# Every third MLP weight unit: its low part summed by an accumulating DMA instead of subtracted on VectorE

## The chip, the cores and the metric

The kernel runs on one core of one Trainium2 chip. The metric is device time of the whole launch in microseconds (us), and a change counts as faster or slower here when the time moves by more than 2%. The core has five engines that run side by side and wait for each other by semaphores: TensorE (PE; its weight loads are listed apart as PEld), VectorE (DVE), ScalarE (ACT), GpSimd (POOL) and SyncE (SP). Sixteen DMA engines move data between HBM and the on-chip SBUF; in this kernel SP issues the weight loads, ACT the results, and POOL a few loads of x.

## The reference

One decoder layer in float32, with 256 tokens and a model width of 2048: an RMS norm and one combined input projection; a causal attention of 8 heads and a gated linear recurrence of 8 heads beside it; sigmoid gates that merge the two; an output projection with a residual; and then the MLP, which is half of all weights:

```python
x = x + merged @ w_out
u = jax.nn.relu(_rmsnorm(x, mlp_norm_g) @ w_mlp1)     # 2048 -> 8192
return x + (u * u) @ w_mlp2                           # 8192 -> 2048
```

All weights are float32, and the result is wanted at about float32 accuracy.

## The kernel before, in words

**The stream of weight units.** All weights are cut into 248 units of 128 x 2048 float32, 1 MB each, that the kernel walks once, in order. Units 0 to 119 belong to the projections; units 120 to 247 are the MLP. The MLP is done in two halves of its width: 32 units of `w1` (120 to 151), 32 of `w2` (152 to 183), 32 of `w1` (184 to 215), 32 of `w2` (216 to 247).

**Two parts of each number.** TensorE multiplies in the type float32r, which keeps fewer bits than float32. So each weight is split in two float32r parts: `hi`, the weight rounded (L110, ScalarE), and `lo`, the weight minus `hi` (L111, VectorE). The activations are held the same way, high and low part side by side in 512 columns (`cat`). A product takes, for each of the 16 blocks of a unit, one matmul of `hi` with all 512 columns and one of `lo` with the 256 high columns (`ws`, L278 to L281). The first block of an accumulation takes `hi` first (L278), then `lo` (L279); the later blocks take `lo`, then `hi` (L281).

**What sets the order.** The function `unit()` hands out unit u and, ahead of that, asks for the load and for the split (`cut`) of unit u+2. `raw`, `hi` and `lo` have three buffers each, so the split of u+2 may write when TensorE has finished with unit u-1, and the load of a unit may start when the split of the unit three before it has read its `raw` buffer. Loads are issued on SP's queue (L90). Each engine runs its instructions in an order that the framework's scheduler fixes when the program is built, and that may differ from the order in which the code is written.

**The MLP beside the matmuls.** In a `w1` unit ScalarE copies the cross terms out of PSUM (`cross`, L292), VectorE adds and applies relu and the norm (L293, L618), ScalarE squares (L620) and rounds the high part (L305), VectorE takes the low part (L306). In the `w2` units VectorE adds the result to the residual (L639, L641, L644). POOL has nothing to do in the MLP.

Of the kernel before, what the change touches and what calls it, by code (L numbers as in the profile page):

```python
# [9 lines left out]
F32 = mybir.dt.float32  # L10
F32R = mybir.dt.float32r
I32 = mybir.dt.int32
AF = mybir.ActivationFunctionType
OP = mybir.AluOpType
AX = mybir.AxisListType

P = 128
T = 256
# [12 lines left out]
def layer_kernel(ctx: ExitStack, tc: tile.TileContext, xT, vecs, wv, wm, wg, wu, wo, w1, w2, cf, cm, out):  # L31
    nc = tc.nc
# [15 lines left out]
    def g4(s, shape=(P, 1024), dt=F32):  # L48
        return gp.tile(list(shape), dt, tag="g", name=uid(s))

    def s1(s, dt=F32, n=256):
        return sp.tile([P, n], dt, tag=f"s{n}", name=uid(s), bufs=6 if n == 256 else 3)

    def bank(s, pool=pp):
        return pool.tile([P, 512], F32, tag="b", name=uid(s))

# [1 line left out]
    units = []  # L58
    for u in range(16):
        units.append(wv[u])  # L60
# [13 lines left out]
    split = {}  # L74
# [3 lines left out]
    def pieces(u):  # L78
        n = 4 if u < 2 else 2 if u < 6 else 1
        w = UW // n  # L80
        return [slice(i * w, (i + 1) * w) for i in range(n)]
# [19 lines left out]
    def cut(u):  # L101
        if u >= len(units):
            return
        hi = wp.tile([P, UW], F32R, tag="hi", name=f"hi{u}")
        lo = wp.tile([P, UW], F32R, tag="lo", name=f"lo{u}")
        raw = raws[u]
        for s in pieces(u):
            if u < 4:
                parts_of_x(range(4 * u + s.start // 512, 4 * u + s.stop // 512))
            nc.scalar.activation(hi[:, s], raw[:, s], AF.Copy)  # L110
            nc.vector.tensor_sub(lo[:, s], raw[:, s], hi[:, s].bitcast(F32))  # L111
        split[u] = (hi, lo)

    AHEAD = 2
# [2 lines left out]
    def unit():  # L117
        u = done[0]
        done[0] += 1
        load(u + AHEAD)  # L120
        cut(u + AHEAD)
        return split.pop(u)

# [1 line left out]
    side = []  # L125
    budget = [0.0]

# [14 lines left out]
                if next(s, None) is None:  # L142
                    side.remove(s)

# [1 line left out]
    NV = 16 + 16 + 32 + 3 + 16  # L146
    vt = cp.tile([P, NV], F32, name="vt")
    nc.scalar.dma_start(vt, vecs)
# [31 lines left out]
    lsc_t = cp.tile([P, 1], F32, name="lsc_t")  # L180
    nc.vector.memset(lsc_t, float(-0.5 * np.log(128.0)))

# [1 line left out]
    xcat = catp.tile([P, KD, 512], F32R, tag="cat", name="xcat")  # L184

    def parts_of_x(ks):
        for k in ks:
            src = xr[k // 4][:, k % 4, :]
            nc.scalar.activation(xcat[:, k, :T], src, AF.Copy, scale=g_in[:, k : k + 1])  # L189
            nc.vector.scalar_tensor_tensor(  # L190
                xcat[:, k, T:], src, g_in[:, k : k + 1], xcat[:, k, :T].bitcast(F32), op0=OP.mult, op1=OP.subtract
            )

    for u in range(2):
        cut(u)

    def rms_rows(ps, dst, n):
        nc.scalar.activation(dst, ps, AF.Sqrt, scale=1.0 / n, bias=eps_t)
        nc.vector.reciprocal(dst, dst)
# [3 lines left out]
    lb = cp.tile([P, 2, NH], F32, name="lb")  # L203

    def prepare():
        """The rms of x over the features, per token: on all partitions, and by partition;
        then the lower bound of the recurrence's gates."""
        acc = g4("acc", (P, 4, T))
        for c in range(4):
            if c == 0:  # L210
                nc.scalar.activation(acc, xr[0], AF.Square)
            else:
                sq = g4("xsq", (P, 4, T))
                nc.scalar.activation(sq, xr[c], AF.Square)
                nc.vector.tensor_add(acc, acc, sq)
            if c % 2:
                yield 1.2 * c
        ssum = cp.tile([P, T], F32, name="ssum")
        nc.vector.tensor_reduce(ssum, acc.rearrange("p k t -> p t k"), axis=AX.X, op=OP.add)
        yield 1.2  # L220
        ps = bank("ps_ss")
        for t in range(2):
            nc.tensor.matmul(ps[:, t : t + 1], ssum[:, t * P : (t + 1) * P], ones[:, :1], start=True, stop=True)
        rms_rows(ps[:, :2], rcol, D)
        ps = bank("ps_ss")
        nc.tensor.matmul(ps[:, :T], ones, ssum, start=True, stop=True)
        rms_rows(ps[:, :T], rstd, D)
        yield 2.2
        lbm = cp.tile([P, NH], F32, name="lbm")
        lbe = cp.tile([P, 2, NH], F32, name="lbe")  # L230
        nc.vector.tensor_max(lbm, lbl[:, 0, :], lbl[:, 1, :])
        for i in range(2):
            nc.vector.tensor_sub(lbe[:, i, :], lbl[:, i, :], lbm)
        nc.scalar.activation(lbe, lbe, AF.Exp)
        nc.vector.tensor_add(lbm, lbe[:, 0, :], lbe[:, 1, :])
        nc.vector.reciprocal(lbm, lbm)
        nc.vector.tensor_mul(lb[:, 0, :], lbe[:, 0, :], lbm)
        nc.vector.tensor_scalar(lb[:, 1, :], lb[:, 0, :], -1.0, 1.0, op0=OP.mult, op1=OP.add)
        yield 1.0

# [1 line left out]
    vv, ii = [[g4(n, (P, 1024)) for _ in range(2)] for n in ("v", "i")]  # L242

    def leave(c, pst):
# [5 lines left out]
    for c in range(4):  # L250
        pst = [bank(f"pv{t}", pm) for t in range(2)]
        for q in range(4):
            hi, lo = unit()
            hi, lo = (x.rearrange("p (k f) -> p k f", k=4) for x in (hi, lo))
# [15 lines left out]
    leave(*full.pop())  # L270

    def ws(parts, pst=None):
        """One tile of features: parts is a list of (hi, lo, cat) 128 x 128 and 128 x 512."""
        pst = pst if pst is not None else bank("pw", pm)
        n = len(parts)
        for i, (h, l, cat) in enumerate(parts):
            if i == 0:
                nc.tensor.matmul(pst, h, cat, start=True, stop=False)  # L278
            nc.tensor.matmul(pst[:, T:], l, cat[:, :T], start=False, stop=False)  # L279
            if i > 0:  # L280
                nc.tensor.matmul(pst, h, cat, start=False, stop=(i == n - 1))  # L281
        return pst

    def unit_parts(hi, lo, cats, off=0):
        return [
            (hi[:, off + k * P : off + (k + 1) * P], lo[:, off + k * P : off + (k + 1) * P], c)
            for k, c in enumerate(cats)
        ]
# [8 lines left out]
    def project(dst):  # L297
        pst = ws(unit_parts(*unit(), xcats))
        s = s1("s")
        summed(pst, s)  # L300
        nc.vector.tensor_mul(dst, s, rstd)

    def to_parts(dst, src, lo_engine=None):
        """dst[..., :n] and dst[..., n:] take the two parts of src."""
        nc.scalar.activation(dst[0], src, AF.Copy)  # L305
        nc.vector.tensor_sub(dst[1], src, dst[0].bitcast(F32))  # L306

# [1 line left out]
    orc = [None] * NH  # L309
    oac = [None] * NH  # L310

# [102 lines left out]
        yield 0.1  # L414

    def head_rms(x, log_scale=0.0):
        """exp(log_scale) / rms over the partitions of x (P, 4, T), on all partitions."""
        sq = g4("sq", (P, 4, T))
        nc.scalar.activation(sq, x, AF.Square)
        yield 0.1  # L420
        sh = g4("sqh", (P, 4, T), F32R)
        nc.scalar.activation(sh, sq, AF.Copy)
        sl = g4("sql", (P, 4, T), F32R)
        nc.vector.tensor_sub(sl, sq, sh.bitcast(F32))
        yield 1.2
        for b in range(2):
            pb = bank("pb")
            hs = slice(2 * b, 2 * b + 2)
            nc.tensor.matmul(pb, ones_r, sh[:, hs, :], start=True, stop=False)  # L429
            nc.tensor.matmul(pb, ones_r, sl[:, hs, :], start=False, stop=True)  # L430
            nc.scalar.activation(
                sq[:, hs, :], pb.rearrange("p (h t) -> p h t", h=2), AF.Ln, scale=1.0 / P, bias=eps_t
            )
        nc.scalar.activation(sq, sq, AF.Exp, scale=-0.5, bias=log_scale)
        yield 0.1
        return sq
# [11 lines left out]
                orc[4 * g + 2 * b + j] = oc[:, j, :]  # L448
        yield 1.2

# [1 line left out]
    shuf = [(i + 16) % 32 for i in range(32)]  # L452

    def rotate(x):
# [92 lines left out]
                step()  # L547
        side.append(attend(g, q, k))

# [1 line left out]
    ga = []  # L551
    for j in range(KD):
        if j % 4 == 0:
# [6 lines left out]
    for j in range(KD):  # L560
# [5 lines left out]
        hi, lo = unit()  # L566
# [5 lines left out]
        a = s1("a")  # L572
# [5 lines left out]
        to_parts((mt[:, j % 2, :T], mt[:, j % 2, T:]), a)  # L578
        mcat.append(mt[:, j % 2, :])

# [1 line left out]
    x2 = []  # L582
    for c in range(4):
        t = g4("x2", (P, 4, T))
# [18 lines left out]
            nc.vector.tensor_add(acc2, acc2, sq)  # L603
    rstd2 = cp.tile([P, T], F32, name="rstd2")

# [1 line left out]
    x2cats = [x2cat[:, k, :] for k in range(KD)]  # L607
    for half in range(2):
        ucat = []
# [15 lines left out]
        for j in range(KD):  # L625
            parts = unit_parts(*unit(), ucat[:16]) + unit_parts(*unit(), ucat[16:])
# [43 lines left out]


def _ws(w):
    """(K, F) as tiles of 128 features: (F / 128, 128 of K, K / 128, 128)."""
    k, f = w.shape
    return np.ascontiguousarray(w.reshape(k // P, P, f // P, P).transpose(2, 1, 0, 3))

# [55 lines left out]
```

## Time and profile before

| | |
|---|---|
| time, two runs | 1456.84 and 1457.02 us, median 1456.93 us |
| profiled execution: span from first to last instruction | 1455.0 us |
| what lies around the span, from the median | 1.9 us |
| granted TensorE clock over the span | 1.000 |
| busy: PE, PEld, DVE, ACT, POOL | 100%, 87%, 62%, 47%, 0% of the span |
| bytes by DMA | 268.14 MB, mean 184 GB/s |
| chain that ended last | PE 99% of it |

The page does not give the profiled execution a time of its own apart from its span; the two timed runs lie 1.8 and 2.0 us above that span. Shares of busy time are taken over the span. The chain is the work followed back from the last instruction: an engine that is not on it can be busy and still cost nothing. An engine's idle time is listed with the instruction that ended it, its releaser.

### The profile page before, as it was taken

The numbers are of one execution on the slowest core, as the hardware profiler recorded it, in microseconds if no ns is written. First come the engines' busy times: TensorE is split into PE (matmuls) and PEld (weight loads), VectorE is DVE, ScalarE is ACT, GpSimd is POOL, SyncE is SP. The second block draws the span as 40 slices with busy tenths as digits, with TensorE's granted clock in tenths as the row PEclk, the third lists the DMA queues.
The fourth block names the chain that finished last, engine by engine and source line by source line (L and its number), as shares of the span: only waits on it lengthen the run. The fifth ranks groups of instructions, "written<-read, shape, count | busy, mean of one in ns | idle before, by whom it ended". The sixth has DMA issues, their size and how long they took to land.

```text
span 1455.0 us, 19682 instructions
## 1 busy us (share of the span) xinstructions
PE 1449.3 (100%) x8336; PEld 1261.7 (87%) x8336; DVE 899.0 (62%) x981; ACT 686.8 (47%) x778; POOL 4.4 (0%) x10
## 2 busy tenths in 40 slices
PE   9999999999999999999999999999999999999999
PEld 7888889888888888888888888888888888888888
DVE  8445776767876766767666666544445666654443
ACT  7444333565755545454455545333335555533331
POOL 0000000000000000000000000000000000000000
PEclk9999999999999999999999999999999999999999
DMA  9554443445444555554555545555545455555551
GB/s 333 204 201 174 173 146 134 156 147 200 150 169 174 173 190 214 190 215 176 192 185 177 200 175 196 179 198 178 198 178 193 183 185 192 177 210 190 208 190 68
DMA packets 41751, 268.14 MB, mean 184 GB/s; under 512 B 4768, under 2 KB 7072, under 8 KB 10688
## 3 DMA queue, kind: packets, MB, share of 16 engines
q1 hardware_dynamic: 38784, 262.78, 50.7%
q0 software_dynamic: 576, 2.10, 0.4%
q10 hardware_dynamic: 2304, 2.01, 0.4%
q8 instruction: 65, 1.06, 0.3%
q14 instruction: 22, 0.18, 0.0%
HBM read 264.78 MB, written 2.10 MB: 183 GB/s over the span
## 4 chain that ended last, share of the span: by engine, by line
PE 99%; DMA 0%; ACT 0%; DVE 0%; issue 0%
PE pw L281 56%; PE pw L279 30%; PE pw L278 3%; PE pv L260 2%; PE pv L262 2%; PE pv L261 2%; PE pd L357 1%; PE pl L485 0%; DMA raw<-wv 0%; PE pw L633 0%; PE pw L631 0%; PE pw L632 0%; PE pd L335 0%; PE pd L365 0%; PE pb L429 0%; PE pb L430 0%
## 5 line engine op out<-in xcount | busy, mean ns | idle before, releaser
L111 DVE TENSOR_TENSOR lo<-raw,hi 128x2048 fp32r<-128x2048 f32 (+2 forms) x258 | 569.3, 2208 | 287.5 <-ACT hi L110 287.3
L110 ACT ACTIVATE hi<-raw 128x2048 fp32r<-128x2048 f32 (+2 forms) x258 | 475.8, 1845 | 306.4 <-PE pw L281 225.6
L281 PE MATMUL pw<-xcat,hi 128*128 128x512 f32 x1080 | 383.6, 397 | 0.0
L281 PE MATMUL pw<-x2cat,hi 128*128 128x512 f32 x960 | 342.4, 399 | 0.0
L281 PE MATMUL pw<-ucat,hi 128*128 128x512 f32 x961 | 337.9, 396 | 0.0
L279 PE MATMUL pw<-xcat,lo 128*128 128x256 f32 x1152 | 311.2, 280 | 0.0
L279 PE MATMUL pw<-x2cat,lo 128*128 128x256 f32 x1024 | 277.2, 281 | 0.0
L279 PE MATMUL pw<-ucat,lo 128*128 128x256 f32 x992 | 271.6, 279 | 0.0
L292 ACT ACTIVATE cross<-pw 128x256 f32<-128x256 f32 x168 | 64.5, 384 | 421.2 <-PE pw L281 421.2
L281 PEld LDWEIGHTS pw<-xcat,hi 128*128 128x128 f32 x1080 | 202.8, 188 | 46.3
L279 PEld LDWEIGHTS pw<-xcat,lo 128*128 128x128 f32 x1152 | 217.5, 189 | 5.2
L281 PEld LDWEIGHTS pw<-ucat,hi 128*128 128x128 f32 x961 | 180.4, 188 | 42.1
L281 PEld LDWEIGHTS pw<-x2cat,hi 128*128 128x128 f32 x960 | 180.4, 188 | 42.0
L279 PEld LDWEIGHTS pw<-x2cat,lo 128*128 128x128 f32 x1024 | 193.5, 189 | 5.5
L279 PEld LDWEIGHTS pw<-ucat,lo 128*128 128x128 f32 x992 | 186.8, 188 | 2.8
L281 PE MATMUL pw<-mcat,hi 128*128 128x512 f32 x240 | 85.6, 399 | 0.0
L293 DVE TENSOR_TENSOR s<-pw,cross 128x256 f32<-128x256 f32 x72 | 30.4, 422 | 76.8 <-ACT cross L292 76.8
L293 DVE TENSOR_TENSOR t<-pw,cross 128x256 f32<-128x256 f32 x64 | 27.2, 426 | 76.3 <-ACT cross L292 76.3
L279 PE MATMUL pw<-mcat,lo 128*128 128x256 f32 x256 | 69.3, 281 | 0.0
L281 PEld LDWEIGHTS pw<-mcat,hi 128*128 128x128 f32 x240 | 45.1, 188 | 10.5
L260 PE MATMUL pv<-hi,xcat 128*128 128x512 f32 x128 | 49.3, 392 | 1.0 <-ACT xcat L189 1.0
L262 PE MATMUL pv<-hi,xcat 128*128 128x512 f32 x128 | 49.8, 389 | 0.0
(185 smaller groups left out, 1198.4 us busy)
## 6 DMA issues: line engine op xcount, KB each, us to landing
raw<-w SPq DMA_DIRECT2D x128, 1024.0 KB, 4.8
raw<-wm SPq DMA_DIRECT2D x56, 1024.0 KB, 4.8
raw<-wg SPq DMA_DIRECT2D x16, 1024.0 KB, 4.8
raw<-wu SPq DMA_DIRECT2D x16, 1024.0 KB, 4.8
raw<-wo SPq DMA_DIRECT2D x16, 1024.0 KB, 4.8
raw<-wv SPq DMA_DIRECT2D x10, 1024.0 KB, 4.8
raw<-wv SPq DMA_DIRECT2D x8, 512.0 KB, 6.9
raw<-wv SPq DMA_DIRECT2D x8, 256.0 KB, 5.1
```

What stands on the lines that cost most here:

```text
L110: nc.scalar.activation(hi[:, s], raw[:, s], AF.Copy)
L111: nc.vector.tensor_sub(lo[:, s], raw[:, s], hi[:, s].bitcast(F32))
L260: nc.tensor.matmul(pst[t], xh, hi[:, k, :], start=(kk == 0), stop=False)
L261: nc.tensor.matmul(pst[t], xh, lo[:, k, :], start=False, stop=False)
L262: nc.tensor.matmul(pst[t], xl, hi[:, k, :], start=False, stop=(kk == KD - 1))
L278: nc.tensor.matmul(pst, h, cat, start=True, stop=False)
L279: nc.tensor.matmul(pst[:, T:], l, cat[:, :T], start=False, stop=False)
L281: nc.tensor.matmul(pst, h, cat, start=False, stop=(i == n - 1))
L292: nc.scalar.activation(c, pst[:, T:], AF.Copy)
L293: nc.vector.tensor_add(dst, pst[:, :T], c)
L357: nc.tensor.matmul(pd[:, i * 64 : (i + 1) * 64].rearrange("p (n j) -> p n j", j=h2), ks[:, h, c], rhs, start=True, stop=True,)
```

## The change

`cut(u)` makes the low part in another way for every third unit of the MLP, u = 120, 123, ..., 246, which are 43 units. ScalarE writes `lo` as the raw weights times -1, rounded to float32r: that is `-hi`. Then a DMA issued by GpSimd reads the raw weights of the unit once more from HBM and adds them to what stands in `lo`. What is left there is the raw weight minus its rounded value, as before. For these units VectorE's subtraction is gone. All other units are cut as before. Some comments are dropped too; the line numbers after the change are 4 higher.

```diff
             nc.scalar.activation(hi[:, s], raw[:, s], AF.Copy)
-            nc.vector.tensor_sub(lo[:, s], raw[:, s], hi[:, s].bitcast(F32))
+            if u >= 120 and u % 3 == 0:
+                nc.scalar.activation(lo[:, s], raw[:, s], AF.Copy, scale=-1.0)
+                nc.gpsimd.dma_start(lo[:, s], units[u][:, s], accum_op=OP.add)
+            else:
+                nc.vector.tensor_sub(lo[:, s], raw[:, s], hi[:, s].bitcast(F32))
         split[u] = (hi, lo)
```

**ScalarE in a `w1` stretch.** Before, the order around the split of unit 132 (the names carry the unit, `hi132`; `cross_576` is the copy-out of unit 129):

```order
L292 ACTIVATE cross_571_6582<-pw_569_6548 128x256
L110 ACTIVATE hi131_6593<-raw131_6591 128x2048
L620 ACTIVATE u2_572_6586<-t_570_6581 128x256
L305 ACTIVATE ucat_573_6588<-u2_572_6586 128x256
L292 ACTIVATE cross_576_6631<-pw_574_6597 128x256
L110 ACTIVATE hi132_6641<-raw132_6639 128x2048
L620 ACTIVATE u2_577_6635<-t_575_6630 128x256
L305 ACTIVATE ucat_573_6588<-u2_577_6635 128x256
```

and the same place after the change:

```order
L296 ACTIVATE cross_571_6586<-pw_569_6552 128x256
L110 ACTIVATE hi131_6597<-raw131_6595 128x2048
L624 ACTIVATE u2_572_6590<-t_570_6585 128x256
L309 ACTIVATE ucat_573_6592<-u2_572_6590 128x256
L112 ACTIVATE lo132_6646<-raw132_6643 128x2048
L296 ACTIVATE cross_576_6635<-pw_574_6601 128x256
L110 ACTIVATE hi132_6645<-raw132_6643 128x2048
L624 ACTIVATE u2_577_6639<-t_575_6634 128x256
L309 ACTIVATE ucat_573_6592<-u2_577_6639 128x256
```

The negated copy (L112) stands ahead of the copy-out of unit 129 and of `hi132`, so `lo132` is written first and `hi132` after it.

**ScalarE in a `w2` stretch**, after the change, around the splits of units 162 and 165 (before, this is a plain row of L110, one for each unit):

```order
L110 ACTIVATE hi160_7959<-raw160_7957 128x2048
L110 ACTIVATE hi161_7965<-raw161_7963 128x2048
L112 ACTIVATE lo162_8039<-raw162_8036 128x2048
L110 ACTIVATE hi162_8038<-raw162_8036 128x2048
L110 ACTIVATE hi163_8045<-raw163_8043 128x2048
L110 ACTIVATE hi164_8118<-raw164_8116 128x2048
L112 ACTIVATE lo165_8125<-raw165_8122 128x2048
L110 ACTIVATE hi165_8124<-raw165_8122 128x2048
```

Here too the negated copy comes ahead of the high part of the same unit.

**GpSimd**, after the change: behind the four loads of x, which it had before, stand the 43 accumulating DMAs and nothing between them:

```order
L589 DMA x2_498_5409<-xT 128x1024
L589 DMA x2_499_5411<-xT 128x1024
L113 DMA lo120_6060<-w1 128x2048
L113 DMA lo123_6207<-w1 128x2048
L113 DMA lo126_6353<-w1 128x2048
```

The order on TensorE is the same as before; its first matmul with `lo` of such a unit now waits for a DMA where it waited for VectorE.

## Rows read from the trace of the kernel before

**Rows 1.** The page: busy us and share of each engine.
```profile
PE 1449.3 (100%) x8336; PEld 1261.7 (87%) x8336; DVE 899.0 (62%) x981; ACT 686.8 (47%) x778; POOL 4.4 (0%) x10
```

**Rows 2.** The page: the chain that ended last, by engine.
```profile
PE 99%; DMA 0%; ACT 0%; DVE 0%; issue 0%
```

**Rows 3.** The MLP as one stretch: length, busy us (instructions), PEclk, DMA share, GB/s.
```profile
core 0: us, PE busy (x) PEld busy (x) DVE busy (x) ACT busy (x) POOL busy (x), PEclk, DMA share, GB/s
735.00:1455.00 720.00, 716.79 (x4109) 624.68 (x4107) 392.03 (x384) 304.75 (x319) 0.00 (x0) 1.00 0.52 183
```

**Rows 4.** The split in the MLP, by line and shape: busy us, mean ns, idle before.
```profile
L111 DVE TENSOR_TENSOR lo<-raw,hi 128x2048 fp32r<-128x2048 f32 x126 | 288.9, 2293 | 194.8 <-ACT hi L110 194.8
...
L110 ACT ACTIVATE hi<-raw 128x2048 fp32r<-128x2048 f32 x125 | 239.1, 1913 | 224.7 <-PE pw L281 222.5 <-issue 2.2
```

**Rows 5.** Timeline of a `w1` stretch, TensorE: start us, us, instruction.
```profile
804.58 0.28 PE L279 MATMUL pw<-x2cat,lo 128*128 128x256 f32 x1
804.94 0.39 PE L278 MATMUL pw<-x2cat,hi 128*128 128x512 f32 x1
810.59 0.39 PE L278 MATMUL pw<-x2cat,hi 128*128 128x512 f32 x1
816.23 0.39 PE L278 MATMUL pw<-x2cat,hi 128*128 128x512 f32 x1
```

**Rows 6.** The same stretch, ScalarE and VectorE.
```profile
805.14 0.39 ACT L292 ACTIVATE cross<-pw 128x256 f32<-128x256 f32 x1 [2.71 <-PE pw L281]
805.42 1.91 ACT L110 ACTIVATE hi<-raw 128x2048 fp32r<-128x2048 f32 x1
807.23 0.40 ACT L620 ACTIVATE u<-t 128x256 f32<-128x256 f32 x1
807.66 0.42 ACT L305 ACTIVATE ucat<-u 128x256 fp32r<-128x256 f32 x1
...
807.36 2.29 DVE L111 TENSOR_TENSOR lo<-raw,hi 128x2048 fp32r<-128x2048 f32 x1 [0.92 <-ACT hi L110]
```

**Rows 7.** Timeline of a `w2` stretch at a unit's border.
```profile
1057.65 0.40 PE L281 MATMUL pw<-ucat,hi 128*128 128x512 f32 x1
...
1057.88 0.40 PE L278 MATMUL pw<-ucat,hi 128*128 128x512 f32 x1
...
1058.08 1.92 ACT L110 ACTIVATE hi<-raw 128x2048 fp32r<-128x2048 f32 x1 [3.73 <-PE pw L281]
...
1058.12 0.39 PE L279 MATMUL pw<-ucat,lo 128*128 128x256 f32 x2
```

**Rows 8.** The page, DMA queues: packets, MB, share of 16 engines' span.
```profile
q1 hardware_dynamic: 38784, 262.78, 50.7%
```

**Rows 9.** The page, DMA issues: line, engine, count, size of one, us to landing.
```profile
raw<-w SPq DMA_DIRECT2D x128, 1024.0 KB, 4.8
...
x<-xT POOLq DMA_DIRECT2D x4, 512.0 KB, 3.6
```

**Rows 10.** POOL's DMAs (tile x): duration ns min/median/max of the issue; then landing.
```profile
L585 POOL DMA_DIRECT2D x<-xT x4: 530/530/664, 508.1 to 636.3; - x4
...
DMA to landing us min/median/max: 3.4/3.6/4.5
```

**Rows 11.** One weight load, us by us, columns as in the rows of the MLP stretch.
```profile
804.00:805.00 1.00, 1.00 (x8) 0.86 (x7) 0.34 (x2) 0.00 (x0) 0.00 (x0) 1.00 0.06 8
805.00:806.00 1.00, 1.00 (x8) 0.87 (x7) 0.42 (x1) 0.86 (x2) 0.00 (x0) 1.00 0.73 147
806.00:807.00 1.00, 1.00 (x7) 0.91 (x6) 0.42 (x1) 1.00 (x1) 0.00 (x0) 1.00 1.05 442
807.00:808.00 1.00, 1.00 (x7) 0.86 (x7) 0.64 (x1) 0.97 (x3) 0.00 (x0) 1.00 0.99 418
808.00:809.00 1.00, 1.00 (x8) 0.86 (x7) 1.00 (x1) 0.08 (x1) 0.00 (x0) 1.00 0.14 49
```

**Rows 12.** Who waited for whom, SP's queue: us in total, times, longest us.
```profile
SPq L90 <- DVE lo L111: 727.9, 137, 11.4
SPq L90 <- DVE ucat L306: 351.9, 63, 6.2
```

## The prediction, made before the changed kernel ran

> **What bounds the kernel now.** I read the totals first, then the chain, then the MLP alone, where the whole change lies. TensorE is busy for 1449.3 of 1455.0 us [rows 1], and 99% of the chain that ended last is TensorE's [rows 2]. In the MLP it is busy 716.79 of 720 us at a granted clock of 1.00, that is 2.4 GHz [rows 3]. VectorE is busy there for 392 us and ScalarE for 305 us, and each spends its idle time waiting for what is ahead of it: the subtraction (L111) waits for the rounding (L110), and the rounding for TensorE [rows 4]. So nothing on VectorE sets the end. The idle time of TensorE in the whole span, 1455.0 - 1449.3 = 5.7 us or 0.4%, is all that relief for another engine can give back. The question is thus only whether the new way delivers `lo` in time; if it does not, TensorE stops at its first matmul with that `lo`, 43 times.
>
> **The time there is.** A unit lasts 5.65 us: TensorE's first matmuls of three units start at 804.94, 810.59 and 816.23 [rows 5]. With three buffers, `lo` of unit u+2 may be written when the last `lo` matmul of unit u-1 has ended, at 804.58 + 0.28 = 804.86 [rows 5], some 0.03 later for the hand-over (the rounding starts at 1058.08, the matmul that frees its buffer ends at 1057.65 + 0.40 [rows 7]). It is needed at the first `lo` matmul of unit u+2, at 816.23 plus the 0.24 between L278 and the first L279 (1057.88 to 1058.12 [rows 7]): 816.47. That is 11.6 us. Before, the rounding and the subtraction of a `w1` unit were done at 807.36 + 2.29 = 809.65 [rows 6], with 6.8 us to spare.
>
> **What is removed.** 43 subtractions of 2.293 us [rows 4], 98.6 us of VectorE. Worth nothing: VectorE is not on the chain.
>
> **What is added on ScalarE.** 43 negated copies. No such row exists; it has the form of the rounding, 128 x 2048 from SBUF to SBUF, so I take its 1.91 us [rows 4, 6]: 82 us on top of 305 of 720. In a `w1` unit ScalarE's work becomes 0.39 + 1.91 + 0.40 + 0.42 + 1.91 = 5.0 us [rows 6], under 5.65. The order shows the copy ahead of `cross` and of `hi`. So those come 1.9 us later: `hi` is done near 804.89 + 1.91 + 0.39 + 1.91 = 809.1, seven us ahead of its use, and the PSUM bank that `cross` empties is one of four. Cost: nothing, covered by that slack. The copy itself ends at 806.80.
>
> **What is added on GpSimd.** Behind the copy, POOL issues the DMA; its queue holds nothing else in the MLP, and an issue takes 0.53 us [rows 10], within the landing time. From 806.83 to 816.47, less a hand-over, **the DMA has 9.6 us from issue to landing.** In a `w2` stretch, when the unit is the second of its pair, `lo` is the first operand and the limit is 0.24 lower.
>
> **What the DMA takes.** No accumulating DMA stands in the trace, so I bound it. The weight loads take 0.507 x 1455.0 = 738 us of all 16 engines for 262.78 MB [rows 8], 2.94 us for 1 MB (1,048,576 bytes), and land after 4.8 us [rows 9]: 1.9 us of latency around the data. POOL's loads of half that size land after 3.6 us [rows 9, 10]: 1.47 of data and 2.1 around them.
> - Lower end: one read, alone: 2.1 + 2.94 = 5.1 us. Hidden by 4.5 us.
> - Two reads: an add needs the raw row from HBM and the standing row from SBUF, so I count the data twice, 5.88 us: 8.0 us alone.
> - Sharing: the weight load three units ahead is issued when `hi` has been written (809.1), 2.3 us behind this DMA. During such a load the DMA engines are full (share 1.05 and 0.99 at 442 and 418 GB/s [rows 11]), so it is not free. If the engines alternate row by row, the accumulating DMA, whose rows take twice as long, gets two thirds: 2.0 us alone, then the remaining 3.9 in 5.8 us, in sum 2.1 + 2.0 + 5.8 = 9.95 us. If the load goes first entirely: 2.1 + 5.88 + 2.94 = 10.95 us.
> - Upper end: two reads and the write one after another, 3 x 2.94 = 8.8 us, behind a load: 2.1 + 8.8 + 2.94 = 13.9 us.
>
> I take 9.95 us, since doubling the reads is the least that an add must do and the rows show both transfers on the same engines. The stall is 9.95 - 9.6 = 0.35 us, times 43 = 15 us. It does not add up from unit to unit, since the next split starts when TensorE moves on. Weight loads that come late cost nothing: issued at 809.1, needed 12.8 us later, when the split of the unit three on starts, they land after 4.8 us, and 5.88 more still fit. SP waits for VectorE before nearly every load [rows 12]; after the change it waits for ScalarE's `hi` (809.1) instead of `lo` (809.65), no later. Over three units (16.9 us) the engines would hold 3 x 2.94 + 5.88 = 14.7 us of data, so they do not saturate.
>
> **Sum:** 1456.9 + 15 = **1472 us**. The terms come from an execution with a span of 1455.0 us; the median 1456.93 lies 1.9 us above it, and I add to the median.
>
> **The skill beside this.** The sharing term rests on the full engines of [rows 11]. The Trainium skill, "DMA: Bandwidth & Descriptors", section "Issuing engines are not separate DMA queues", says the same against this change: DMAs of any issuing engine run on the same 16 and interleave. Were it otherwise, 8.0 us would be hidden and the sum 1457 us. For the price of the add only a page has figures: the Trainium skill, "Collectives: The Full Stack", section "The bandwidth ceiling: the fold count and why AG ≠ RS ≠ AR", says that a reducing DMA runs at half the copy's rate because it reads two sources, not because the add costs cycles, with about 31 GB/s read by one engine. By its figures an estimate is 1,048,576 x 2 / (16 x 31,000) = 4.2 us of data, 8.3 to 9.3 us with latency and load, and the sum would be 1457 us. No run here shows it yet.
>
> **Rivals.**
> 1. *The add costs more than two reads* (slower). Place: the wait of TensorE's first `lo` matmul on POOL's DMA. It decides from 9.6 us on, and 2% (29 us, 0.68 us a unit) is passed at 10.3. Ends: 10.95 us gives 43 x 1.35 = 58, 1515 us; 13.9 us gives 43 x 4.3 = 185, 1642 us. For it: the limit sits right at my estimate, and casting into float32r or a longer issue on POOL would each push it over. Against: only 14.7 of 16.9 us of engine time asked. 0.28.
> 2. *Rows are not overlapped* (much slower). 128 rows on 16 engines are 8 each; if each row waited for its own write, with 2.1 us each and the data of 2.94, 20 us: 43 x 10.4 = 447, 1904 us. The loads overlap theirs, which speaks against it, but an add must read, then write the same place. 0.19 for all above 14 us.
> 3. *Hidden altogether*: one read counts, or the load does not disturb: 1457 us. It is one case with my forecast, since less than 2% parts them; together 0.51, with a range of their own from 1452 to 1486 us.
> 4. *Faster*: only if matmuls themselves got shorter with VectorE quieter, since waits hold 0.4% at most. Nothing in the rows points to it: 0.02.
>
> **Range and chances.** Differences under 2%, about 29 us, count as no change. Low end 1450 us: the 5.7 us of idle time returned. High end 1640 us: rival 1 to its upper end; only rival 2 (0.19) and a little of rival 4 lie outside. Faster 0.02, same 0.51, slower 0.28 + 0.19 = 0.47.
>
> **What the profile after would show.** Right: POOL's 43 DMAs land some 10 us after issue, a quarter of DMA-engine time more in the MLP, L112 near 1.91 us, TensorE idle before L283 waiting for DMA for under 0.5 us each, clock still 1.00. Rival 1 or 2: the landing time above 10.3 us, TensorE's idle time near 43 times the excess. Rival 3: landing under 9.6 us and no wait of TensorE. The prediction is wrong in its first step if TensorE waits on ScalarE (`hi` or L112) instead, or if SP's loads come late and L110 waits for `raw`.

## The result, and the profile after

The changed kernel takes 1471.09 us (two runs, 1468.84 and 1473.33) against 1456.93 us: a ratio of 1.0091, 95% interval 1.0075 to 1.0107. That is slower beyond the noise and under the 2% that count as a change. The forecast was 1472 us. In the profiled execution (1468.84 us) the span is 1467.1 us, 12.1 us longer than before.

The page's totals, against [rows 1]:

```profile
PE 1455.2 (99%) x8336; PEld 1259.3 (86%) x8336; DVE 802.1 (55%) x938; ACT 763.8 (52%) x821; POOL 41.5 (3%) x53
```

VectorE lost 97 us and ScalarE gained 77 us, and neither shows in the time. The MLP as one stretch, against [rows 3]; the columns are the same:

```profile
735.00:1467.00 732.00, 722.95 (x4111) 622.47 (x4109) 297.71 (x342) 380.19 (x361) 36.16 (x42) 1.00 0.80 240
```

It is 12.0 us longer, which is the whole loss; the clock stays at 1.00. TensorE's idle time grew by 5.8 us only (720 - 716.79 before, 732 - 722.95 now) and its busy time by 6.2 us for the same matmuls. A matmul that waits at its start is partly drawn as a longer one: the longest `lo` matmul is 388 ns beside a median of 281. So the loss is read from the length of the stretch, not from the idle time. Who waited, TensorE's matmuls and its weight loads (us in total, times, longest); the two overlap and don't add up, and 39 of the 43 units have a weight load that waits:

```profile
PE pw L283 <- DMA lo<-w: 5.7, 11, 1.0
```
```profile
PEld pw L283 <- DMA lo<-w: 18.2, 39, 1.4
```

The new DMA, from the page's queues and issues, then from the list of its line (issue in ns, then landing in us):

```profile
q1 hardware_dynamic: 38784, 262.78, 48.6%
q0 software_dynamic: 6768, 47.19, 17.3%
...
raw<-w SPq DMA_DIRECT2D x128, 1024.0 KB, 5.8
...
lo<-w POOLq DMA_DIRECT2D x43, 1024.0 KB, 9.2
```
```profile
L113 POOL DMA_DIRECT2D lo<-w x43: 848/860/887, 722.3 to 1443.3; - x43
...
DMA to landing us min/median/max: 8.2/9.2/10.4
```

It lands after 8.2 to 10.4 us; six of the 43 land later than the 9.6 us that the prediction set as the limit. One late unit in the timeline, against [rows 5, 6]: ScalarE's copy, POOL's issue, TensorE's first matmuls of four units, its first `lo` matmul and the weight load ahead of that:

```profile
805.43 1.92 ACT L112 ACTIVATE lo<-raw 128x2048 fp32r<-128x2048 f32 x1 [2.50 <-PE pw L283]
...
807.64 0.85 POOL L113 DMA_DIRECT2D lo<-w  x1 [16.12 <-ACT cross L296]
...
805.47 0.39 PE L282 MATMUL pw<-x2cat,hi 128*128 128x512 f32 x1
811.11 0.39 PE L282 MATMUL pw<-x2cat,hi 128*128 128x512 f32 x1
816.76 0.39 PE L282 MATMUL pw<-x2cat,hi 128*128 128x512 f32 x1
817.84 0.51 PE L283 MATMUL pw<-x2cat,lo 128*128 128x256 f32 x2 [0.69 <-DMA lo<-w]
823.37 0.39 PE L282 MATMUL pw<-x2cat,hi 128*128 128x512 f32 x1
...
817.84 0.30 PEld L283 LDWEIGHTS pw<-x2cat,lo 128*128 128x128 f32 x2 [1.12 <-DMA lo<-w]
```

The copy starts 0.04 us before TensorE's first matmul of the unit two before (805.47), as forecast. POOL starts 0.29 us after the copy's end (805.43 + 1.92 = 807.35). The data are there after 10.2 us, and the first `lo` matmul, due at 816.76 + 0.24 = 817.00, starts 0.84 us late. (The page names `cross` as POOL's releaser here; L112, which the DMA needs, ended just before it.) The unit takes 823.37 - 816.76 = 6.61 us instead of 5.65, so it loses 0.96 us.

The first reader of `lo` is not the matmul but the weight load ahead of it, and that one starts with the unit's first matmul. In the kernel before (816.23 in [rows 5]):

```profile
816.24 0.41 PEld L279 LDWEIGHTS pw<-x2cat,lo 128*128 128x128 f32 x2
```

So a landing that costs nothing has to come near the start of the unit, 9.1 to 9.2 us after the issue and not 9.6. A unit with a usual landing, after 9.3 us (issue at 773.61), loses 0.2 us: it takes 788.49 - 782.65 = 5.84 us.

```profile
782.65 0.39 PE L282 MATMUL pw<-x2cat,hi 128*128 128x512 f32 x1
788.49 0.39 PE L282 MATMUL pw<-x2cat,hi 128*128 128x512 f32 x1
...
782.96 0.30 PEld L283 LDWEIGHTS pw<-x2cat,lo 128*128 128x128 f32 x2 [0.35 <-DMA lo<-w]
```

The stretch of the late unit us by us, with the columns of [rows 11]:

```profile
807.00:808.00 1.00, 1.00 (x8) 0.86 (x7) 0.35 (x1) 1.00 (x3) 0.36 (x1) 1.00 1.02 434
...
809.00:810.00 1.00, 1.00 (x7) 0.91 (x6) 0.00 (x0) 0.97 (x3) 0.00 (x0) 1.00 1.03 98
810.00:811.00 1.00, 1.00 (x7) 0.86 (x7) 0.43 (x1) 0.17 (x1) 0.00 (x0) 1.00 0.74 147
811.00:812.00 1.00, 1.00 (x8) 0.87 (x7) 0.27 (x1) 0.69 (x2) 0.00 (x0) 1.00 0.84 164
812.00:813.00 1.00, 1.00 (x8) 0.86 (x7) 0.58 (x2) 1.00 (x1) 0.00 (x0) 1.00 1.23 254
```

At 807 a plain load fills the engines and moves 434 GB/s. From 809 on the accumulating DMA has them, at nearly the same share, and 98 to 164 GB/s land: the last column counts what is moved to its place, not what is read for it (queue q0 moves 47.19 MB with the add, and 47.19 MB without it in the run with one read). From 812 the next load is mixed in.

### The profile page after: what moved, and what is told of

The parts are those of the page before. It is cut to its first block, busy times and chain, and to the rows that moved or that the text cites. A ratio compares the mean times of both kernels' runs of the same rounds, so it can differ in the third digit from the quotient of the medians.

```text
span 1467.1 us, 19773 instructions
## 1 busy us (share of the span) xinstructions
PE 1455.2 (99%) x8336; PEld 1259.3 (86%) x8336; DVE 802.1 (55%) x938; ACT 763.8 (52%) x821; POOL 41.5 (3%) x53
## 3 DMA queue, kind: packets, MB, share of 16 engines
q0 software_dynamic: 6768, 47.19, 17.3%
## 5 line engine op out<-in xcount | busy, mean ns | idle before, releaser
L115 DVE TENSOR_TENSOR lo<-raw,hi 128x2048 fp32r<-128x2048 f32 (+2 forms) x215 | 470.7, 2191 | 257.0 <-ACT hi L110 256.9
L110 ACT ACTIVATE hi<-raw 128x2048 fp32r<-128x2048 f32 (+2 forms) x258 | 475.0, 1843 | 193.6 <-PE pw L285 99.2
L112 ACT ACTIVATE lo<-raw 128x2048 fp32r<-128x2048 f32 x43 | 82.4, 1916 | 138.1 <-PE pw L283 138.1
L643 DVE TENSOR_TENSOR x<-pw,x 128x256 f32<-128x256 f32 x31 | 13.2, 425 | 104.0 <-PE pw L285 104.0
L113 POOL DMA_DIRECT2D lo<-w x43 | 37.0, 862 | 770.0 <-ACT lo L112 443.3
```

The source lines that it names most:

```text
L112: nc.scalar.activation(lo[:, s], raw[:, s], AF.Copy, scale=-1.0)
L113: nc.gpsimd.dma_start(lo[:, s], units[u][:, s], accum_op=OP.add)
L643: nc.vector.tensor_add(d, pst[:, :T], d)
```

## The experiments

Theory A: the loss is TensorE's wait for a DMA whose chain (copy, issue, two reads, a weight load beside it) is about as long as the lead of 11.5 us. The rivals say that the loss is contention that slows TensorE with or without a wait (B), that the price is in POOL's path or the cast and not in the second read (C), or that the load beside costs nothing (D). Times are medians; "before" is the kernel before, run on the same chip: 1457.10 us beside the first four, 1458.70 beside all units, 1458.19 beside the last two.

**The wait taken away, all traffic kept.**

```diff
+                if late[b // 16]:
+                    seq += [("h", i) for i in range(b, b + 16)] + [("l", i) for i in range(b, b + 16)]
...
-            pst = ws(unit_parts(*unit(), x2cats))
+            at = done[0]
+            pst = ws(unit_parts(*unit(), x2cats), late=[at % 3 == 0])
...
-            pst = ws(parts)
+            pst = ws(parts, late=[at % 3 == 0, (at + 1) % 3 == 0])
```

> All DMAs, copies and traffic of the change are kept; only TensorE's order inside the 43 units is other: the 16 matmuls with hi first, then the 16 with lo, so that lo is needed some 3.5 us later. Theory A (the loss is TensorE's wait for a DMA that lands late): the DMA still takes 9 to 10 us to landing, TensorE waits for it no more, and the time is that of the kernel before, 1457 us within 4. Rival B (the added DMA and ScalarE traffic slows TensorE or its feeders by contention, with or without a wait): the loss stays, 1466 to 1472 us.

Measured: 1455.31 us, ratio to before 0.9989 (0.9979 to 0.9998). TensorE waits for no DMA in the MLP, though the DMA lands later than ever:

```profile
DMA to landing us min/median/max: 8.8/10.6/11.5
```
```profile
735.00:1453.20 718.20, 714.96 (x4116) 626.92 (x4114) 297.86 (x342) 383.95 (x361) 36.17 (x42) 1.00 0.85 245
```

All copies, all DMAs and a DMA share of 0.85, and no loss: B falls, and the loss is the wait. (Unit 246, in the last tile, keeps its order, so 42 units have the new one. That order gains some 0.045 us a unit by itself, as the last run but one shows, which is about the 1.8 us by which this run lies below the kernel before; next to nothing is left for contention.)

One thing besides the order moved. TensorE is now done with `hi` earlier in these units, so ScalarE writes `hi` ahead of the negated copy. The load that waits until `raw` has been read is then issued 0.27 us before the DMA (POOL starts at 807.52), where it was issued 1.80 us behind it in the changed kernel (POOL at 807.64). This run first, then the changed kernel:

```profile
807.26 0.33 SPq L90 DMA_DIRECT2D raw<-w  x1
```
```profile
809.44 0.33 SPq L90 DMA_DIRECT2D raw<-w  x1
```

So the DMA meets the whole load, which goes with the later landing.

**One read instead of two.**

```diff
-                nc.gpsimd.dma_start(lo[:, s], units[u][:, s], accum_op=OP.add)
+                nc.gpsimd.dma_start(lo[:, s], units[u][:, s])
```

> The DMA copies the raw weights over lo instead of adding them (accumulate left out, so the product is another one); copy on ScalarE, issue on POOL and everything else stay. Theory A with its price of two reads: engine time of POOL's queue falls from 5.8 to about 2.9 us for 1 MB, landing from 9.2 to 6 or 7 us, no wait, 1457 us within 3. Rival C (the price is in POOL's path, in the cast or in latency, not in the second read): landing stays at 8.5 us or more and the time at 1464 us or more.

Measured: 1457.74 us, ratio 1.0001 (0.9991 to 1.0010), and no wait. The queue and the line:

```profile
q0 software_dynamic: 6768, 47.19, 9.4%
```
```profile
L113 POOL DMA_DIRECT2D lo<-w x43: 527/527/530, 722.2 to 1431.2; - x43
...
DMA to landing us min/median/max: 4.9/5.2/6.5
```

Less the 0.4% of POOL's loads of x, the queue's engine time is 9.0% of 1455.2 us or 3.0 us for each of 43, against 16.9% of 1467.1 or 5.8 us with the add: a factor of 1.9. C falls, with a remainder: POOL's issue of an add takes 0.86 us instead of 0.53, which is 0.33 of the 4.0 us between the two landings. The 5.2 us is the prediction's lower end (5.1). The run takes away the add as a whole; it does not part the second read from the adding itself. The factor agrees with a rule of the Trainium skill, "Collectives: The Full Stack", section "The bandwidth ceiling: the fold count and why AG ≠ RS ≠ AR", by which a reducing DMA is slower for its two source reads and not for the add.

**No load beside it.**

```diff
+            if u >= 123 and u % 3 == 0:
+                nc.sync.dma_start(raws[u][:, :128], units[u][:, :128])
...
+                few = raw[:, None, :128].to_broadcast([P, 16, 128])
```

> The weight load that runs beside each accumulating DMA is cut to a sixteenth (of units 123, 126, ... only 128 columns are loaded, and ScalarE reads these 16 times over; the result is another one). Theory A with its sharing term: landing falls from 9.2 to 8.0 to 8.4 us, below the limit of about 9.3, and the time to 1457 us within 3. Rival D (sharing costs nothing, the add alone takes 9 us): landing stays near 9.2 and the time at 1466 us or more.

Measured: 1460.24 us, ratio 1.0017 (1.0007 to 1.0027).

```profile
DMA to landing us min/median/max: 7.9/8.1/10.7
```
```profile
PEld pw L292 <- DMA lo<-w: 2.8, 5, 1.7
```

Landing alone is 8.1 us, where 8.0 was forecast; sharing adds 1.1 us to the median. D falls. The time did not come back entirely, against theory A's 1457 within 3: a few DMAs still landed late, up to 10.7 us, with five waits. The trace shows what ran beside those few. Seven DMAs land after 8.8 us or more, and in the flight of each of them the engines moved one 16 KB packet of the program's instructions (queue q8); of the other 35, seven had one. From 1095.3 to 1104.5 us, where a DMA lands after 9.2:

```profile
q8 instruction: 1, 0.02, 0.6%
```

In the changed kernel all six that land after 9.8 us or more had such a packet, and 11 of the other 37. This is a coincidence in time; no run took these packets away.

**A longer chain.**

```diff
                 nc.scalar.activation(lo[:, s], raw[:, s], AF.Copy, scale=-1.0)
+                nc.scalar.activation(lo[:, s], lo[:, s].bitcast(F32), AF.Copy)
```

> ScalarE copies lo onto itself once more ahead of the DMA. By the order of its instructions the DMA then starts about 4.5 us later in w1 units (copy, cross, hi, square, second copy) and 3.7 us later in w2 units (copy, hi, second copy). Theory A (a chain of copy, issue and landing against a fixed lead of 11.5 us): nearly all of it becomes TensorE idle time, 43 x 4.1 on top, 1620 to 1650 us. Rival B (contention, not the chain): 82 us more of ScalarE time off the path, 1470 to 1476 us.

Measured: 1650.61 us (two runs), ratio 1.1325 (1.1294 to 1.1356). The number is A's, its make-up is not. The span is 190.3 us longer than before; TensorE's listed waits are 122.9 us, 2.9 for each unit, since the DMA now starts behind the load and lands after 8.0 us. Most of the rest is the clock, whose mean in the MLP is 0.93: 7% of 910.3 us are 64 us.

```profile
PE pw L284 <- DMA lo<-w: 120.5, 42, 4.2
PE pw L637 <- DMA lo<-w: 2.4, 1, 2.4
```

One wait and what followed, from windows of 1 us (PEclk is the last but two):

```profile
1012.00:1013.00 1.00, 0.40 (x3) 0.08 (x1) 0.00 (x0) 0.56 (x1) 0.00 (x0) 1.00 1.22 254
1013.00:1014.00 1.00, 0.00 (x0) 0.00 (x0) 0.00 (x0) 1.00 (x1) 0.00 (x0) 1.00 0.84 188
1014.00:1015.00 1.00, 0.24 (x2) 0.25 (x3) 0.62 (x1) 0.35 (x1) 0.00 (x0) 1.00 0.99 410
1015.00:1016.00 1.00, 1.00 (x6) 0.84 (x6) 1.00 (x1) 0.00 (x0) 0.00 (x0) 0.73 1.02 434
1016.00:1017.00 1.00, 1.00 (x5) 0.81 (x4) 0.67 (x1) 0.00 (x0) 0.00 (x0) 0.50 0.38 156
```

After an idle stretch of 2.35 us the granted clock falls from 2.4 to 1.2 GHz, when the matmuls already run again, and at 1019 it is back. Not every wait is followed by this: TensorE idles for 2.7 us up to 842.7, and the clock stays.

```profile
841.00:842.00 1.00, 0.00 (x0) 0.00 (x0) 0.08 (x2) 1.00 (x2) 0.00 (x0) 1.00 0.97 205
...
844.00:845.00 1.00, 1.00 (x7) 0.87 (x6) 0.59 (x2) 0.00 (x0) 0.00 (x0) 1.00 0.55 229
```

34 stretches of half clock stand behind the 43 waits. In the profiled execution of the changed kernel, where the longest wait of a weight load is 1.4 us, it stays at 1.00.

**All units.**

```diff
-            if u >= 120 and u % 3 == 0:
+            if u >= 120:
```

> All 128 MLP units take the accumulating DMA. Theory A plus engine time (2.9 us for the load and 5.8 for the add in each unit, 8.7 of DMA-engine time against 5.65 of TensorE): the DMA engines become the bound, 128 x 3.1 = 390 us more, about 1850 us, DMA share near 1.0 in the MLP. Rival E (only each unit's own latency counts, the engines have room): as now in every unit, 128 x 0.3 = 40 us, about 1495 us.

Measured: 1690.83 us (two runs), ratio 1.1593 (1.1559 to 1.1627).

```profile
735.00:1688.40 953.40, 768.09 (x4109) 634.86 (x4107) 109.74 (x256) 529.88 (x445) 107.73 (x125) 0.97 1.02 278
```

The DMA engines are full (1.02), so E falls and the bound is the one expected; its price was too high by two thirds (390 us for 232). 278 GB/s land in two transfers per unit, and if the add is counted as two reads, 1.5 x 278 = 417 GB/s are read, near the 442 GB/s of a plain load [rows 11]. So a MB read costs 2.5 us of full engines (1,048,576 / 417,000), not the 2.94 us that I took from the queue's share: that share counts the time of each packet, waiting included, and goes over 1 (1.23 above). Three reads are 7.5 us for a unit, 1.9 over TensorE's 5.65, times 128 is 240 us; measured were 232. That the two agree tests nothing, since the 2.5 us come from the length of this same run; with the 442 GB/s of a plain load it would be 2.37 us for a MB and 187 us.

**TensorE's order alone, in the kernel before.** The run with the wait taken away was 1.8 us below the kernel before. This one has no accumulating DMA and the grouped order in every feature tile.

```diff
-        for i, (h, l, cat) in enumerate(parts):
-            if i == 0:
-                nc.tensor.matmul(pst, h, cat, start=True, stop=False)
-            nc.tensor.matmul(pst[:, T:], l, cat[:, :T], start=False, stop=False)
-            if i > 0:
-                nc.tensor.matmul(pst, h, cat, start=False, stop=(i == n - 1))
+        for b in range(0, n, 16):
+            for i, (h, l, cat) in enumerate(parts[b : b + 16]):
+                nc.tensor.matmul(pst, h, cat, start=(b + i == 0), stop=False)
+            for i, (h, l, cat) in enumerate(parts[b : b + 16]):
+                nc.tensor.matmul(pst[:, T:], l, cat[:, :T], start=False, stop=(b + i == n - 1))
```

> The kernel before, without any accumulating DMA, with TensorE's order changed in all feature tiles: the 16 matmuls with hi of a unit, then the 16 with lo. It asks where the 1.8 us come from by which the run with lo last in 43 units lies below the kernel before. Theory F (the grouped order is itself shorter, 0.04 us a unit): some 230 units have it, 9 us less, about 1448 us. Rival G (it comes from VectorE's relief, 99 us less work, or is noise): no gain here, 1457 us within 2.

Measured: 1445.17 us, ratio 0.9916 (0.9902 to 0.9929): F, and faster than both kernels. TensorE's timeline:

```profile
800.85 3.82 PE L278 MATMUL pw<-x2cat,hi 128*128 128x512 f32 x16
804.50 2.08 PE L280 MATMUL pw<-x2cat,lo 128*128 128x256 f32 x16
806.41 3.82 PE L278 MATMUL pw<-x2cat,hi 128*128 128x512 f32 x16
```

A `w1` unit takes 806.41 - 800.85 = 5.56 us instead of 5.65. Elsewhere the gain is smaller (a `w2` unit took 5.60 us before and takes 5.57): the span is 1455.0 - 1444.7 = 10.3 us shorter, 0.045 us for each of the 230 units.

**The changed kernel again.**

> The changed kernel as it is, in more executions, on the chip of the run beside it. Theory A (a wait of 0 to 1.2 us in each of 43 units, by where the weight load falls): 1468 to 1474 us with a spread of a few us, wider than that of the kernel before. If the two first executions were not typical: below 1464 or above 1478 us.

Measured: 1472.51 us (four runs, 1468.91 to 1474.94), ratio 1.0099 (1.0083 to 1.0114). The spread of 6 us is wider than that of the kernel before (1456.68 to 1458.79); the landing times are 8.0 to 10.7 us. The two longest of the four also show a granted clock of 0.997 and 0.999 over the span; 0.3% of 1473 us are 4 us, so part of this spread is the clock.

## Why the prediction was right

- **The bound.** TensorE alone sets the end; relief of VectorE was worth nothing. Shown by the run with one read: TensorE's order and 97 us less VectorE work as in the changed kernel, no wait, and 1457.74 us beside 1457.10.
- **The lead of 11.5 us, given by three buffers.** Shown in the main: the copy starts 0.04 us before the unit two before, and a longer chain costs time at once. But the end of the lead was set at the first `lo` matmul, 0.24 us after L282; its weight load reads `lo` first, near the start of the unit.
- **Two reads.** Right in size: 8.1 us alone for 8.0 forecast, 5.2 with one read for 5.1. That the price is a second read, and not the adding, is argued, not shown.
- **Sharing.** Right in kind, too large: 1.1 us instead of 1.95, so the median landing is 9.2 us and not 9.95. The engine time of 2.94 us for 1 MB fits a DMA by itself (with 2.5 us the 8.0 would have been 7.1), but it is too much for full engines, which take 2.5 us: a load that runs beside the whole DMA adds 10.6 - 8.1 = 2.5 us (the run with the wait taken away). It also made the expectation for all units 160 us too high. That both transfers go over the same engines was read into rows that don't show it; the loads of `w` beside the DMAs show it, landing after 5.8 us instead of 4.8.
- **The limit.** 0.4 us too late. The weight load takes 0.2 of it, the handover the rest: POOL starts 0.29 us after ScalarE's copy, not 0.03, and its issue takes 0.86 us, not 0.53 (this lies within the landing time). So 9.1 to 9.2 us were left from the issue, and the median landing is right there.
- **The stall.** Not 0.35 us in every unit. The mean is 12.1 / 43 = 0.28 us in the profiled execution. Six late landings cost 0.6 to 1.25 us each, 5.8 us together; the other 37 units share the remaining 6 us, and among them the `w2` units whose `lo` is the first operand lose 0.1 to 0.5 us each. The sum, 12 to 16 us, fits the forecast of 15, and part of this is luck: the landing was put 0.6 us too late (9.95 for a mean of 9.3), the limit 0.4 us too late, and the two errors partly cancel. The spread around the limit, which makes half of the loss, was not in the prediction.
- **The estimate by the Trainium skill's figures** ("Collectives: The Full Stack", the section named above). The 8.3 to 9.3 us by 31 GB/s read by one engine contain the median landing of 9.2; that they would all be hidden, and the time 1457 us, failed because the limit was 9.1 to 9.2 us, and by the late landings. The 31 GB/s itself is not what full engines do here: 417 GB/s in the run with all units are 26 GB/s for each of 16 engines, and the measurement decides.
- **Rivals.** Rival 1 lies where the change would cross over: its condition, a landing above 9.6 us, holds for six units of 43. Rival 2 is excluded by the 8.1 us landing alone. Rival 3 would have landings under 9.6 us and no wait; 37 units land so, and most of them wait. Rival 4 finds nothing in the run with one read. A landing later by 0.4 us in every unit would have passed the 2%, so the class was a close call, as its chance of 0.51 said.

## What to carry to other kernels

Before work is moved from an idle-enough engine to a DMA, compare the whole new chain (write, handover, issue, every read the DMA makes, the transfers it will meet) with the lead that the buffers give; here a subtraction with 6.8 us to spare became a chain with none. When a median lands right at a deadline, the spread of the landings is the price. If a late operand can't be made earlier, let the consumer use it later: the order of the matmuls removed the wait, and cost nothing.

## What the runs showed of the hardware that was not expected

- With full engines, and an add counted as two reads, accumulating and plain DMAs together read 417 GB/s, beside 442 for a load alone.
- After a wait of 2.35 us the granted clock fell to 0.50, and only after the matmuls had begun again; after another of 2.7 us it stayed at 1.00.
- The first reader of a weight is TensorE's weight load: it started at 816.24 where the matmul that uses it started at 816.46, so an operand is late 0.2 us earlier than the matmuls show.
- The late landings of accumulating DMAs coincide with 16 KB packets of instructions: seven of seven without a load beside them, six of six in the changed kernel. It was not tested.
- Sixteen 512-column matmuls in a row and then sixteen of 256 columns take 5.56 us in a `w1` unit, the same ones alternating 5.65 us; over the kernel this is worth 0.8%. Why the alternating order costs more was not examined.
